# In-projection with a 512-column moving operand in the first and last token block

## The chip, the cores and the metric

The kernel runs as one program on one core of a Trainium2 chip. The metric is the device time of one execution in microseconds (us). The kernel before takes 2049.98 us, the median of three runs (2048.39 to 2051.28). One more execution was recorded by the hardware profiler, and all durations below are from that one.

## The reference

The reference is one transformer block on 2048 tokens of width 1024, with 256 context tokens. What matters here is its first part: the normed and modulated tokens are multiplied by one wide matrix `w_in`, and the product is split into eight pieces.

```python
hx = modulate(rmsnorm(x, norm1_w), sh1, sc1)
aq, ak, av, mq, mk, mv, mo, gates = jnp.split(h @ w_in, offs, -1)
mqk = jax.nn.silu(short_conv(jnp.concatenate([mq, mk], -1), conv_qk))
```

`aq`, `ak`, `av` feed a windowed attention (8 heads of 64, window 128, plus the context tokens), `mq`, `mk`, `mv`, `mo` and the gates feed a linear recurrence over chunks in both directions. Behind these come the output projection and a mixture of 16 experts of which each takes its best 256 tokens.

## The kernel before

The kernel has three stages, one behind the other: in-projection with attention (`phase_in`), recurrence with output projection (`phase_mix`), and experts (`phase_moe`). The change touches the first one alone.

**Tokens.** The tokens are worked through in four blocks of 512, and a block is two units of 256 tokens, `("x", 2b)` and `("x", 2b+1)`. The context is one more unit, worked through beside block 0. A unit's activations are held transposed (model dimension on the partitions) as two fp32r tiles of 8 x 256 columns, a rounded part `hx_hi` and the rest `hx_lo`. There are three slots for units (`self.hxs`); a unit takes the slot that came free first (`hxslot`). The units of block 0 get slots 0 and 1, those of block 1 slots 2 and 0, of block 2 slots 1 and 2, and of block 3 slots 0 and 1 again. In the kernel before each slot is a pair of tiles of its own (`hx_pair`).

**Weights.** `w_in` is loaded 128 columns at a time (L721), split by ACT into `w_hi` (L735) and by DVE into `w_lo` (L741). Each product is hi*hi, hi*lo and lo*hi, so 3 x 8 matmuls per output tile.

**Two kinds of chain.** Where the output is wanted with tokens on the partitions (`kv`, `q`, `mv`, `mo`), `tok_chain` (L758) keeps the activations stationary and moves 256 or 272 weight columns. Where it is wanted with channels on the partitions (`mk`, `mq`, which the convolution runs along the tokens), `chan_chain` (L776) keeps 128 x 128 of the weights stationary and moves the tokens of a unit, 256 columns. It does so for one unit, then for the other, into the two halves of one PSUM tile `mm` of 512 columns. So each stationary piece is loaded twice, once per unit. A block has 8 such chains for its two units (4 groups of 2), and block 0 has 4 more for the context unit. Their output goes through the convolution and a SiLU (`conv_out`).

**Order.** Nothing is left to the compiler's scheduling. All work of the stage is written as generators that ask for an engine with a cost in us (`yield "P", CH * 0.108` asks TensorE for four matmuls), and `Flow.run` plays them against one clock per engine and takes the waiting task of best priority. What comes out is a fixed sequence of instructions per engine. The engines then run their sequences strictly in that sequence and wait for each other by semaphores. The projection (`main`) has the last priority on TensorE, so that attention scores (L258, L262), transposes (L303), and values (L331, L332) are put in wherever the planner's clock says that their input is there. Planned costs of other engines are `A(n)` = 0.085 + 0.00085 n for ACT and `V(n)` = 0.07 + 0.00105 n for DVE, n being the columns.

Of the kernel before, what the change touches and what calls it, by code (L numbers as in the profile page):

```python
# [22 lines left out]
F32R = mybir.dt.float32r  # L23
# [12 lines left out]
KT = D // 128  # L36
# [320 lines left out]
class Kernel:  # L357
# [69 lines left out]
    def phase_in(self):  # L427
        nc, tc = self.nc, self.tc
        with ExitStack() as st:
            pool = lambda name, bufs, **k: st.enter_context(tc.tile_pool(name=name, bufs=bufs, **k))  # L430
            self.ps = pool("psin", 1, space=PSUM)
            self.right, self.mod, self.att = ExitStack(), ExitStack(), ExitStack()
            self.keep = self.outer.enter_context(tc.tile_pool(name="gkeep", bufs=1, side="right"))
            self.hxp = self.right.enter_context(tc.tile_pool(name="hxp", bufs=2, side="right"))
            self.hxs = [self.hx_pair(self.hxp, i) for i in range(2)]
            self.early = ExitStack()
            self.ep = self.early.enter_context(tc.tile_pool(name="early", bufs=1, side="right"))
            self.wp = pool("wring", 1)
            self.w_hi = self.wp.tile([128, 4, KT, 136], F32R, name="w_hi")
            self.w_lo = self.wp.tile([128, 4, KT, 136], F32R, name="w_lo")  # L440
            self.mp = self.mod.enter_context(tc.tile_pool(name="mod", bufs=1))
            self.pool = pool
            fl = self.fl = Flow()
            self.bufs, self.alt = BUFS, {}
            self.tok = {n: Tokens(k) for n, k in BUFS.items()}
            self.tok["hx"], self.tok["slot"] = Tokens(2), Tokens(4)
            self.hxslot = [0, 1, 2]
            self.hx = {}
            units = [("x", 0), ("x", 1), ("c", 0)] + [("x", i) for i in range(2, 8)]
            self.wm_ev = [Event() for _ in range(KT)]  # L450
            self.xn = {u: Event() for u in units}
            self.hx_ev = {u: Event() for u in units}
            self.hh_ev, self.hl_ev = ({u: [Event() for _ in range(4)] for u in units} for _ in range(2))
            self.order = {u: n for n, u in enumerate(units)}
            self.hx_freed = {u: Event() for u in units}
            self.mod_ev, self.opened, self.main_done, self.rest_ev, self.turned = (Event() for _ in range(5))
            self.att_ev, self.gt_ev = Event(), Event()
            self.reach = {(b, g): Event() for b in range(4) for g in GROUPS}
            self.w_ev = [Event() for _ in range(88)]
            self.kt_ev = [Event() for _ in range(NT)]  # L460
            self.ckt_ev = [Event() for _ in range(2)]
            self.q_ev = {(n, i): Event() for n in range(NT) for i in range(2)}
            self.unit_done = [Event() for _ in range(NT)]
            self.g_ev = Event()
            self.g_left = NT + 2
            self.q2t, self.carry = {}, {}
            fl.spawn(self.load_x(units), PRI["loadx"])
            fl.spawn(self.mod_first(), PRI["mod1"])
            for u in units:
                fl.spawn(self.make_hx(u), PRI["hx"])  # L470
            fl.spawn(self.weights(), PRI["w"])
            fl.spawn(self.main(), PRI["main"])
            self.uns = [Unit(self, n, kv) for n in range(NT) for kv in range(2)]
            fl.spawn(self.scores_flow(), PRI["sc"])
            fl.spawn(self.trans_flow(), PRI["tr"])
            fl.spawn(self.values_flow(), PRI["val"])
            fl.spawn(self.mod_rest(), PRI["modr"])
            fl.spawn(self.gates(), PRI["gates"])
            fl.run()
            self.early.close()  # L480
            self.right.close()
# [282 lines left out]
    def chan_chain(self, sl, units):  # L764
        yield self.tok["mm"]
        ps = self.buf(self.ps, "mm", [128, 512])
        for j, u in enumerate(units):
            hi, lo, _ = self.hx[u]
            i = 0
            for w, hx, evs in ((self.w_hi, hi, self.hh_ev), (self.w_hi, lo, self.hl_ev), (self.w_lo, hi, self.hh_ev)):  # L770
                for k in range(KT):
                    if k % CH == 0:
                        for ev in evs[u][k // 2:(k + CH + 1) // 2]:
                            yield ev
                        yield "P", CH * 0.108
                    self.nc.tensor.matmul(ps[:, j * 256:(j + 1) * 256], lhsT=w[:, sl, k, 0:128], rhs=hx[:, k, :],  # L776
                                          start=(i == 0), stop=(i == 23))
                    i += 1
        return ps
# [1998 lines left out]
```

## Time and profile before

| | |
|---|---|
| Median of three runs | 2049.98 us |
| Profiled execution, its own time | 2041.91 us |
| Its span, first to last instruction | 2040.1 us |
| TensorE busy | 1854.6 us (91%) |
| VectorE (DVE) busy | 1597.8 us (78%) |
| ScalarE (ACT) busy | 1281.9 us (63%) |
| GpSimd (POOL) busy | 855.1 us (42%) |
| In-projection and attention | about 44 to 910 us of the span |
| Recurrence and output projection | about 910 to 1490 us |
| Experts | about 1490 to 2040 us |

The profiled execution took 8.07 us less than the median of the runs. Busy is a sum over instructions, with overlaps counted once; matmuls are pipelined, and the end of one is modelled, so the start of one to the start of the next tells their pace better than their length. An engine's idle time costs something only where it delays the chain of work that ends last.

### The profile page before, as it was taken

The page shows a single profiled execution, that of the slowest core. Times are in us where ns is not written, and L with a number is a line of the kernel's source. Part 1 is how long each engine was busy: PE and PEld are TensorE (multiplying, and loading weights), DVE is VectorE, ACT ScalarE, POOL GpSimd, SP SyncE. Part 2 cuts the span into 40 slices and gives each one's busy share as a digit, 9 for nine tenths or more (in the row PEclk, how much of TensorE's full clock was granted, in tenths as well). Part 3 has the DMA queues.
Part 4 walks back from the last instruction along what each step waited for, and adds up shares of the span by engine and source line. Part 5 has one row for each costly group of instructions (what it writes and reads, how often), then busy time and mean ns, then how long its engine had stood idle before and what let it go on. Part 6 is the DMA issues. An engine that isn't in the chain of part 4 may idle for free.

```text
span 2040.1 us, 36979 instructions
## 1 busy us (share of the span) xinstructions
PE 1854.6 (91%) x12921; PEld 1657.3 (81%) x12921; DVE 1597.8 (78%) x3470; ACT 1281.9 (63%) x3136; POOL 855.1 (42%) x828
## 2 busy tenths in 40 slices
PE   8799999999999999987989798993499999999997
PEld 2698998899889989985777576782399999999996
DVE  3799789998998799868999777756777878787772
ACT  3567777777787777775656488864355545454542
POOL 0324324433443243225778765413244535353532
PEclk9899999999999999997999899996699999999999
DMA  8343264445432333237878677636277878878772
GB/s 281 101 146 102 71 194 119 126 139 152 114 108 79 94 83 102 77 99 226 267 254 274 237 252 242 220 132 240 74 232 216 262 222 257 238 235 253 225 230 42
DMA packets 293498, 357.81 MB, mean 175 GB/s; under 512 B 27288, under 2 KB 225592, under 8 KB 292416
## 3 DMA queue, kind: packets, MB, share of 16 engines
q1 hardware_dynamic: 283072, 320.32, 49.7%
q0 software_dynamic: 9376, 34.08, 7.2%
q8 instruction: 102, 1.67, 0.4%
q10 hardware_dynamic: 864, 1.05, 0.1%
q14 instruction: 84, 0.69, 0.1%
HBM read 270.73 MB, written 84.54 MB: 174 GB/s over the span
## 4 chain that ended last, share of the span: by engine, by line
PE 58%; DVE 21%; ACT 7%; DMA 6%; issue 5%; POOL 1%; SPq 0%; POOLq 0%; DVEq 0%; ACTq 0%
PE gu L2637 18%; PE mm L758 9%; PE yp L2689 8%; PE po L2002 5%; DVE w_lo L741 3%; DMA w_raw<-in_w_in 2%; PE t L303 2%; PE h L1910 2%; PE s L258 2%; PE o L593 1%; PE o L332 1%; PE t L2581 1%; PE o L331 1%; ACT w_hi L735 1%; PE h L1622 1%
## 5 line engine op out<-in xcount | busy, mean ns | idle before, releaser
L2486 ACT ACTIVATE ew_hi<-ew_raw 128x1024 fp32r<-128x1024 f32 x192 | 202.1, 1056 | 155.7 <-PE yp L2689 91.7
L2446 DVE TENSOR_TENSOR ew_lo<-ew_raw,ew_hi 128x1024 fp32r<-128x1024 f32 x152 | 217.5, 1440 | 33.2 <-issue 17.9
L291 POOL TENSOR_SCALAR P<-P,am 128x640 f32<-128x640 f32 (+1 forms) x128 | 112.8, 881 | 258.5 <-DVE am L289 147.7
L741 DVE TENSOR_TENSOR w_lo<-w_raw,w_hi 128x256 fp32r<-128x256 f32 (+1 forms) x352 | 156.9, 471 | 30.5 <-ACT w_hi L735 28.6
L2709 POOL DMA_INDIRECT out_x<-y,idx x32 | 57.1, 1786 | 271.0 <-DVE y L2703 183.8
L2637 PE MATMUL gu<-xg_hi,ew_hi 128*128 128x256 f32 x1024 | 148.5, 283 | 0.0
L735 ACT ACTIVATE w_hi<-w_raw 128x256 fp32r<-128x256 f32 (+1 forms) x352 | 134.9, 410 | 19.8 <-DMA w_raw<-in_w_in 19.0
L758 PE MATMUL mm<-w_hi,hx_hi 128*128 128x256 f32 (+1 forms) x944 | 142.7, 289 | 4.8 <-ACT hxr L933 2.2
L758 PE MATMUL mm<-w_lo,hx_hi 128*128 128x256 f32 (+1 forms) x944 | 141.2, 286 | 0.0
L758 PE MATMUL mm<-w_hi,hx_lo 128*128 128x256 f32 (+1 forms) x944 | 140.9, 287 | 0.0
L2637 PE MATMUL gu<-xg_hi,ew_lo 128*128 128x256 f32 x1024 | 140.8, 279 | 0.0
L2637 PE MATMUL gu<-xg_lo,ew_hi 128*128 128x256 f32 x1024 | 140.7, 279 | 0.0
L758 PEld LDWEIGHTS mm<-w_hi,hx_hi 128*128 128x128 f32 x944 | 125.0, 190 | 9.1 <-ACT hxr L933 2.6
L2637 PEld LDWEIGHTS gu<-xg_hi,ew_hi 128*128 128x128 f32 x1024 | 131.2, 189 | 0.1
L2637 PEld LDWEIGHTS gu<-xg_hi,ew_lo 128*128 128x128 f32 x1024 | 128.4, 188 | 0.0
L2637 PEld LDWEIGHTS gu<-xg_lo,ew_hi 128*128 128x128 f32 x1024 | 128.4, 188 | 0.0
L758 PEld LDWEIGHTS mm<-w_hi,hx_lo 128*128 128x128 f32 x944 | 124.0, 189 | 3.3 <-issue 2.6
L758 PEld LDWEIGHTS mm<-w_lo,hx_hi 128*128 128x128 f32 x944 | 124.3, 189 | 1.8 <-issue 0.9
L314 DVE TENSOR_TENSOR pl<-t,ph 128x512 fp32r<-128x512 f32 x156 | 105.8, 684 | 24.3 <-ACT ph L312 23.0
L282 ACT ACTIVATE P<-s,am 128x640 f32<-128x640 f32 (+1 forms) x128 | 99.8, 780 | 31.0 <-DVE am L280 25.6
L2703 DVE SCALAR_TENSOR_TENSOR y<-yp,gv,g2b 128x512 f32<-128x512 f32 x64 | 48.0, 751 | 89.8 <-PE yp L2689 89.8
L280 DVE CUSTOM_DVE_ANT_0 s<-s,mrow,nsink 128x640 f32<-128x640 f32 (+1 forms) x120 | 105.3, 878 | 12.9 <-PE s L262 6.6
(480 smaller groups left out, 5613.0 us busy)
## 6 DMA issues: line engine op xcount, KB each, us to landing
w_raw<-in_w_in SPq DMA_DIRECT2D x176, 256.0 KB
ew_raw<-in_w_gate SPq DMA_DIRECT2D x32, 1024.0 KB
ew_raw<-in_w_up SPq DMA_DIRECT2D x32, 1024.0 KB
ew_raw<-in_w_down SPq DMA_DIRECT2D x32, 1024.0 KB
xt<-in_w_mod SPq DMA_DIRECT2D x64, 256.0 KB
out_x<-xl SPq DMA_DIRECT2D x32, 512.0 KB
s_vs<-vsl SPq DMA_DIRECT2D x16, 516.0 KB
vsl<-s_vs SPq DMA_DIRECT2D x16, 516.0 KB
```

What stands on the lines that cost most here:

```text
L280: nc.vector.tensor_tensor_reduce(x, x, mask, 1.0, k.nsink[:, h:h + 1], op0=OP.add, op1=OP.min, accum_out=m[:, 0:1])
L282: nc.scalar.activation(P[:, :n], sc, AF.Exp, bias=m[:, 0:1], scale=-1.0, accum_out=m[:, 1:2])
L291: nc.gpsimd.tensor_scalar(P[:, :n], P[:, :n], m[:, 4:5], 0.0, op0=OP.mult, op1=OP.add)
L314: nc.vector.tensor_sub(lo, pt, f(hi))
L735: nc.scalar.activation(hi, raw[:, k:k + 2, :n], AF.Copy)
L741: nc.vector.tensor_sub(lo, raw[:, k:k + 2, :n], f(hi))
L758: self.nc.tensor.matmul(ps[:, :2 * n].rearrange("p (a b) -> p a b", a=2), lhsT=hx[:, k, t * 128:(t + 1) * 128], rhs=w[:, sl:sl + 2, k, :n] ...
L2002: self.nc.tensor.matmul(po, lhsT=m[:, k, :], rhs=self.wo[k0 + k][wi][:, sl], start=(j == 0), stop=(j == 11))
L2446: (self.nc.vector if eng == "D" else self.nc.gpsimd).tensor_sub(out, x, y)
L2486: nc.scalar.activation(hi[:, sl], raw[:, sl], AF.Copy)
L2637: nc.tensor.matmul(po[:, ft, :], lhsT=w[:, k, ft * 128:(ft + 1) * 128], rhs=x[:, k, :], start=(j == 0), stop=(j == 23))
L2689: nc.tensor.matmul(po[hf], lhsT=hs[i][h][:, ft, t * 128:(t + 1) * 128], rhs=wd[i][w][:, ft, hf * 512:(hf + 1) * 512], start=(j[hf] == 0), ...
```

## The change

The two slots 0 and 1 become one tile, `hx01`, indexed by slot, by part (0 is hi, 1 is lo), by k and by token; `self.hxs` holds views of it, so all writers and the other chains work as they did. `chan_chain` gets a branch for the case that its two units sit in slots 0 and 1, which is so in block 0 and block 3. There one matmul moves 512 columns, 256 from each slot, over one stationary piece: 24 matmuls of 512 columns in place of 48 of 256. The planner is asked for two such matmuls at a time at a cost of 0.46 us, where it was asked for four at 4 x 0.108 = 0.432 us, and each group waits for the activations of both units. Blocks 1 and 2 and the context unit take the old branch.

```diff
-            self.hxs = [self.hx_pair(self.hxp, i) for i in range(2)]
+            self.hx01 = self.hxp.tile([128, 2, 2, KT, 256], F32R, name="hx01", bufs=1)
+            self.hxs = [(self.hx01[:, i, 0], self.hx01[:, i, 1]) for i in range(2)]
...
         ps = self.buf(self.ps, "mm", [128, 512])
+        if [self.hx[u][2] for u in units] == [0, 1]:
+            i = 0
+            for w, j, evs in ((self.w_hi, 0, self.hh_ev), (self.w_hi, 1, self.hl_ev), (self.w_lo, 0, self.hh_ev)):
+                for k in range(KT):
+                    if k % 2 == 0:
+                        for u in units:
+                            yield evs[u][k // 2]
+                        yield "P", 0.46
+                    self.nc.tensor.matmul(ps.rearrange("p (a b) -> p a b", a=2), lhsT=w[:, sl, k, 0:128],
+                                          rhs=self.hx01[:, :, j, k, :], start=(i == 0), stop=(i == 23))
+                    i += 1
+            return ps
```

Since the costs enter the planner's clock, the sequences of all engines change from the first such chain on, to the end of the stage. The two later stages keep their sequences. Lines below the branch stand 13 lines further down in the changed kernel, those between the two edits one line further.

TensorE at the first channel chains of block 0. `hx_hi` and `hx_lo` are the parts of a unit (the number behind them is the builder's: 96 and 97 unit x0, 98 and 99 unit x1, 386 and 387 the context), `mm` the PSUM tile, `hxr` and `gate` what is transposed for keys and gates. Before:

```order
L776 MATMUL mm<-hx_hi_96,w_hi 128x256 x8
L776 MATMUL mm<-hx_lo_97,w_hi 128x256 x8
L1056 MATMUL tr<-cst,hxr_734 128x128
L1057 MATMUL tr<-cst,gate 8x128
L1058 MATMUL tr<-cst,gate 8x128
L776 MATMUL mm<-hx_hi_96,w_lo 128x256 x8
L776 MATMUL mm<-hx_hi_98,w_hi 128x256 x8
L776 MATMUL mm<-hx_lo_99,w_hi 128x256 x8
L776 MATMUL mm<-hx_hi_98,w_lo 128x256 x8
L776 MATMUL mm<-hx_hi_386,w_hi 128x256 x8
```

The same place in the changed kernel, where `hx_96` is the joint tile and 383 and 384 are the context:

```order
L776 MATMUL mm<-hx_96,w_hi 128x512 x8
L1069 MATMUL tr<-cst,hxr_731 128x128
L1070 MATMUL tr<-cst,gate 8x128
L1071 MATMUL tr<-cst,gate 8x128
L776 MATMUL mm<-hx_96,w_hi 128x512 x8
L776 MATMUL mm<-hx_96,w_lo 128x512 x8
L789 MATMUL mm<-hx_hi_383,w_hi 128x256 x8
```

Six groups of eight matmuls of 256 columns became three groups of eight of 512. The key transposes stand behind as many projected columns as before.

TensorE later in block 0, at the first scores over three key tiles (L258 with 384 columns), that is of the attention's second tile of 128 queries. Before:

```order
L758 MATMUL mm<-w_hi,hx_lo_99 128x256 x4
L996 MATMUL tr<-cst,hxr_1804 128x128 x2
L758 MATMUL mm<-w_hi,hx_lo_99 128x256 x4
L758 MATMUL mm<-w_lo,hx_hi_98 128x256 x8
L258 MATMUL s<-kt,q2t 128x384 x2
L262 MATMUL s<-ckt,q2t 128x256 x2
L758 MATMUL mm<-w_hi,hx_hi_386 128x256 x8
```

And in the changed kernel:

```order
L789 MATMUL mm<-hx_lo_384,w_hi 128x256 x4
L1009 MATMUL tr<-cst,hxr_1685 128x128 x2
L789 MATMUL mm<-hx_hi_383,w_lo 128x256 x8
L759 MATMUL mm<-w_hi,hx_96 128x256 x8
L258 MATMUL s<-kt,q2t 128x384 x2
L262 MATMUL s<-ckt,q2t 128x256 x2
L759 MATMUL mm<-w_hi,hx_96 128x256 x8
```

Before, this score stands in the `mv` chains of unit x1, and 912 projection matmuls of 256 columns stand ahead of it in the row; in the changed kernel it stands in those of unit x0, and 824 stand ahead, a matmul of 512 columns counted as two.

TensorE at the end of the stage; L1449 (L1462 in the changed kernel) is the first matmul of the next stage. Before:

```order
L303 MATMUL t<-cst,P 128x128 x4
L331 MATMUL o<-ph,vt 128x512
L332 MATMUL o<-pl,vt 128x512
L303 MATMUL t<-cst,P 128x128 x4
L758 MATMUL mm<-w_lo,hx_hi_98 128x256 x8
L331 MATMUL o<-ph,cvt 128x512
L332 MATMUL o<-pl,cvt 128x512
L331 MATMUL o<-ph,cvt 128x512
L332 MATMUL o<-pl,cvt 128x512
L1449 MATMUL t<-wr,sh_82 1x16 x8
```

In the changed kernel:

```order
L759 MATMUL mm<-w_lo,hx_96 128x256 x4
L331 MATMUL o<-ph,cvt 128x512
L332 MATMUL o<-pl,cvt 128x512
L759 MATMUL mm<-w_hi,hx_96 128x256 x16
L759 MATMUL mm<-w_lo,hx_96 128x256 x8
L759 MATMUL mm<-w_hi,hx_96 128x256 x16
L759 MATMUL mm<-w_lo,hx_96 128x256 x8
L1462 MATMUL t<-wr,sh_82 1x16 x8
```

Before, the last values of the attention end the row; in the changed kernel 48 projection matmuls (the last two `mo` chains) stand behind them.

## Rows read from the trace of the kernel before

**Rows 1.** The page's head and its summary of engines: busy time, share of the span, instructions.

```profile
span 2040.1 us, 36979 instructions
PE 1854.6 (91%) x12921; PEld 1657.3 (81%) x12921; DVE 1597.8 (78%) x3470; ACT 1281.9 (63%) x3136; POOL 855.1 (42%) x828
```

**Rows 2.** Busy time of each engine in stretches of the stage, cut by token block (95 to 310, 310 to 521, 521 to 722 and 722 to 910 us); columns as in the first line.

```profile
core 0: us, PE busy (x) PEld busy (x) DVE busy (x) ACT busy (x) POOL busy (x), PEclk, DMA share, GB/s
95.00:310.00 215.00, 206.49 (x1621) 196.08 (x1620) 182.77 (x477) 155.98 (x427) 71.72 (x114) 1.00 0.44 129
310.00:521.00 211.00, 199.98 (x1540) 186.69 (x1541) 193.44 (x504) 160.50 (x430) 80.23 (x106) 1.00 0.46 131
521.00:722.00 201.00, 193.34 (x1496) 183.30 (x1495) 171.66 (x457) 158.67 (x429) 77.72 (x105) 1.00 0.36 100
722.00:910.00 188.00, 181.05 (x1376) 168.58 (x1374) 161.94 (x451) 143.69 (x371) 60.51 (x93) 1.00 0.29 83
```

**Rows 3.** The same view for the two stretches in which the channel chains of blocks 0 and 3 run (95 to 178 and 722 to 809 us) and for the rest of these blocks.

```profile
95.00:178.00 83.00, 78.03 (x631) 73.65 (x630) 77.31 (x197) 58.56 (x161) 27.96 (x50) 1.00 0.47 136
178.00:310.00 132.00, 128.46 (x993) 122.43 (x992) 105.47 (x281) 97.42 (x268) 43.77 (x64) 1.00 0.42 124
...
722.00:809.00 87.00, 83.17 (x653) 77.41 (x651) 83.84 (x239) 67.02 (x175) 31.30 (x49) 1.00 0.36 100
809.00:910.00 101.00, 97.88 (x723) 91.17 (x723) 78.10 (x214) 76.67 (x196) 29.21 (x44) 1.00 0.23 68
```

**Rows 4.** The chain of work that ended last, its shares by line: in 95 to 178 us, in 722 to 809 us, and in 809 to 910 us.

```profile
by line: DVE w_lo L741 16.6%; issue 9.8%; DMA s_mq<-cv 8.2%; DMA xt<-in_x 5.3%; ACT w_hi L735 5.2%; DVE cv L876 4.1%; DMA w_raw<-in_w_in 3.9%; DVE cv L874 3.4%; DVE s L280 2.6%; DVE cu L549 2.4%; ACT cu L543 2.4%; ACT cu L545 2.3%; DVE cv L
...
by line: PE mm L776 13.7%; DVE w_lo L741 11.8%; issue 11.0%; DVE cv L876 4.7%; DVE s L280 4.1%; DVE pl L314 3.5%; DVE q2t L1006 3.5%; ACT w_hi L735 3.2%; DVE grow L1277 3.1%; ACT P L282 2.9%; DVE cv L874 2.7%; DVE cu L549 2.0%; DVE am L287 
...
by line: PE mm L758 34.9%; PE t L303 13.0%; PE s L258 8.5%; PE o L331 7.1%; PE o L332 6.9%; DMA s_att<-cv 5.5%; PE s L262 5.2%; DMA w_raw<-in_w_in 3.4%; issue 2.7%; ACT P L282 1.9%; ACT w_hi L735 1.4%; DVE w_lo L741 1.3%; ACT cv L347 1.2%; 
```

**Rows 5.** What TensorE waited for, all of 44 to 910 us: total, times, longest.

```profile
PE s L258 <- ACT P L282: 7.9, 14, 1.4
...
PE o L332 <- DVE pl L314: 4.3, 8, 1.0
PE tr L996 <- DVE q2t L1006: 4.2, 4, 2.5
```

**Rows 6.** All channel-chain matmuls, by part: count, ns of one (least, median, most), first and last start.

```profile
L776 PE MATMUL mm<-hx_hi,w_hi x544: 274/280/387, 95.2 to 806.6; 128*128 128x256 f32 x182
L776 PE MATMUL mm<-hx_lo,w_hi x544: 275/280/388, 96.2 to 807.5; 128*128 128x256 f32 x182
L776 PE MATMUL mm<-hx_hi,w_lo x544: 274/280/388, 98.7 to 808.7; 128*128 128x256 f32 x182
```

**Rows 7.** TensorE in order of time: start, length, instructions merged. Channel chains of 256 columns in block 0, with nothing between them.

```profile
99.73 1.11 PE L776 MATMUL mm<-hx_hi,w_hi 128*128 128x256 f32 x8
...
105.38 1.10 PE L776 MATMUL mm<-hx_hi,w_hi 128*128 128x256 f32 x8
```

**Rows 8.** The same view, matmuls of 512 columns: in this stage (attention values), in the next one (output projection), and in the experts (24 in a row, the first and the last shown).

```profile
906.70 0.39 PE L331 MATMUL o<-ph,cvt 128*128 128x512 f32 x1
906.94 0.40 PE L332 MATMUL o<-pl,cvt 128*128 128x512 f32 x1
907.17 0.39 PE L331 MATMUL o<-ph,cvt 128*128 128x512 f32 x1
907.40 0.43 PE L332 MATMUL o<-pl,cvt 128*128 128x512 f32 x1
...
945.42 1.10 PE L2002 MATMUL po<-wo_hi,mixh 128*128 128x512 f32 x4
946.36 1.09 PE L2002 MATMUL po<-wo_hi,mixl 128*128 128x512 f32 x4
...
1813.81 0.39 PE L2689 MATMUL yp<-ew_hi,h_hi 128*128 128x512 f32 x1
...
1819.02 0.39 PE L2689 MATMUL yp<-ew_lo,h_hi 128*128 128x512 f32 x1
```

**Rows 9.** The same view, token chains, whose moving operand of 256 columns is read in two pieces of 128.

```profile
785.58 1.11 PE L758 MATMUL mm<-w_hi,hx_lo 128*128 128x256 f32 x8
...
787.49 1.11 PE L758 MATMUL mm<-w_hi,hx_hi 128*128 128x256 f32 x8
```

**Rows 10.** Groups of DVE and ACT instructions over 60 to 920 us: line, engine, operation, shapes, count, busy us, mean ns of one, idle time before them.

```profile
L741 DVE TENSOR_TENSOR w_lo<-w_raw,w_hi 128x256 fp32r<-128x256 f32 x312 | 139.2, 472 | 11.8 <-ACT w_hi L735 10.0
L735 ACT ACTIVATE w_hi<-w_raw 128x256 fp32r<-128x256 f32 x312 | 118.8, 409 | 15.7 <-DMA w_raw<-in_w_in 14.9
```

**Rows 11.** The chain that ended last, at the end of the stage: start, us, what.

```profile
905.91 0.97 PE mm L758 x8
906.90 0.40 ACT moe L912
...
908.30 0.60 ACT cv L347
...
909.73 5.56 DMA s_att<-cv
```

## The prediction

> **What bounds the kernel now.** I read the page's summary first: over the whole span TensorE is the busiest engine, 1854.6 of 2040.1 us, with VectorE behind it at 1597.8 [rows 1]. An average over three stages says little about one of them, so I next cut the in-projection by token blocks [rows 2]. In all four blocks TensorE is busy 95 to 96% of the time, and the granted clock is 1.00, the 2.4 GHz level; what it is not busy is 8.5 us in block 0, 11.0 in block 1, 7.7 in block 2 and 6.95 in block 3. So over a block TensorE is the bound, and a matmul saved is worth something as long as the idle time does not grow in its place.
>
> Inside blocks 0 and 3 the picture splits [rows 3]. While the channel chains run, DVE is as full as TensorE: 77.3 against 78.0 of 83 us in block 0, and 83.8 against 83.2 of 87 us in block 3. In the rest of the blocks TensorE is busy 97% and DVE 77 to 80%. The chain of waits says the same thing [rows 4]. In the channel stretch of block 0 the channel matmuls L776 are not among its large shares at all; the weight split on DVE leads with 16.6%. In that of block 3 they have 13.7%, which is 11.9 of 87 us. In the last stretch TensorE's lines lead, L758 alone with 34.9%. So the matmuls that the change touches stand mostly beside work of DVE that ends later. Their saving shows up only by letting TensorE reach the later work, where it is the bound, sooner.
>
> **The change part by part.** *Fewer, wider matmuls.* There are 544 x 3 = 1632 channel matmuls [rows 6]. Of these 4 x 24 = 96 are the context's, and 1536 are the four blocks', 384 each. Blocks 0 and 3 have 768, which become 384 of 512 columns; 384 weight loads go with them. Columns stay the same. From start to start a 256-column matmul of these chains takes (105.38 - 99.73) / 48 = 0.1177 us [rows 7], two of them 0.2354. For 512 columns there are three rows [rows 8]: the values in this stage (907.40 - 906.70) / 3 = 0.2333 us; the output projection (946.36 - 945.42) / 4 = 0.235 us; the experts (1819.02 - 1813.81) / 23 = 0.2265 us. None of them reads its 512 columns in two pieces. The token chains read theirs in two, and take (787.49 - 785.58) / 16 = 0.1194 us [rows 9], 0.0017 more than a channel matmul. Best end: the experts' pace and no surcharge, 0.2354 - 0.2265 = 0.0089 us a pair, times 384 = 3.4 us gained. Worst end: the output projection's pace with the surcharge, 0.2367, 0.5 us lost. The values are the nearest row by their surroundings, the experts by their form (a long run, each with weights of its own), so I take the middle of those two, 0.230, with the surcharge: 0.2316, 0.0038 us a pair, 1.5 us gained.
>
> The weight loads that go are not on the path by these rows: all 512-column rows have one load each and still run near twice the pace of 256. The Trainium skill says more than one thing of this ("TensorE: Matmul & The Clock Gate", section "Back-to-back issue gap"): an isolated gap of N/2.4 + 2.5 ns, by which a pair would gain 2.5 ns and the change 1.0 us, and a sustained 131 ns per matmul of 512 columns in a stream of load and matmul pairs. The trace contradicts the second: none of the 512-column paces above is under 226 ns. The first agrees with it in size only: 256 columns take 117.7 ns here, where it gives 109.
>
> *The joint tile.* It takes the room of the four tiles, and its writers write the same slices. Waits that would tie slot 0's writers to slot 1's readers cost nothing in blocks 0 and 3, where both slots are filled before the chains start; block 1 and 2 fill one of them while the other is read. I take nothing for it, as every write into a slot stands in the sequence behind the chains that planned to free it; were this wrong it would add to TensorE's waits of [rows 5], and belongs to the slower rival's price.
>
> *Waiting for both units.* A group now needs hi or lo of both. The `kv` and `q` chains of both units stand ahead of the first channel chain, so both have been read in full by then: nothing.
>
> *Another sequence.* This is the larger term, and its sign is open. A channel chain was planned at 48 x 0.108 = 5.18 us and ran 48 x 0.1177 = 5.65; it is now planned at 24 x 0.23 = 5.52 and would run 24 x 0.2316 = 5.56. The planner thus sees TensorE later than it did by 0.34 us a chain, 5.4 us over 16 chains, and puts attention work in ahead of more projection. The score shown in the change stands behind 824 projection matmuls, not 912, and at the stage's end 48 stand behind the last values, where none stood. Does that cost idle time? The four blocks are four sequences of much the same work, and their idle times [rows 2] have a mean of 8.5 and a standard deviation of 1.8 us. If all four are drawn anew the sum moves by 3.6 us (1.8 times the root of 4). I take zero, with that spread. No DMA is added or dropped, and on SP's queue the weight loads (w_raw) keep their places among the other transfers but for a few, so nothing is taken for them; they end 3.9% of the chain in block 0's stretch [rows 4].
>
> *The stage's end.* Before, the end runs from the last token chain (905.91 + 0.97) over the sigmoid and the values' store to 909.73, and the store takes 5.56 us more, after which loads of the next stage are free to go [rows 11]. Now `mo` chains end the row. Their sigmoid starts on ACT right behind the chain, as in those rows, and their store some 3 us behind it, as the values' store does there. The values' store then lies some 48 x 0.1194 = 5.7 us ahead of the end and no longer ends it: between 0 and 2 us gained, taken as nothing since a store ends the stage either way.
>
> Sum: -1.5 us. The profiled execution's own 2041.91 would be 2040.4. It stood 8.07 us under the median of the runs, so the sum is carried to the median as a difference: 2049.98 - 1.5 = 2048.5 us.
>
> **The rivals.** *Slower: attention comes too early for DVE.* The planner's DVE is too fast: a weight split is planned at 0.07 + 256 x 0.00105 = 0.34 us and takes 0.472, on ACT 0.30 and 0.409 [rows 10]. Before, TensorE's plan for these chains was too fast as well, by 9%, and this hid the error. Now it is nearly right, and attention pieces stand up to 88 matmuls earlier, 88 x 0.1177 = 10.4 us, while DVE has 83 - 77.3 = 5.7 us to spare in block 0. In block 3, with the 48 matmuls of the end as the measure, 5.7 us against 3.2 to spare. What DVE can't take, 4.7 + 2.5 = 7.2 us, becomes waits of TensorE at L258, L332 and L996, the places where it waits for ACT and DVE now [rows 5], with the projection queued behind them. Then 7.2 - 1.5 = +5.7 us: 2055.7. It decides from 5.6 us more waits on, where 1.5 us are paid back and 4.1 remain. Against it: longest waits there are 1.0 to 2.5 us now, and projection pieces stand between.
>
> *Faster: the sequence fits better.* Since TensorE's plan now holds in these stretches, ACT and DVE meet it where they expect it. If blocks 0 and 3 lost half of their 8.5 + 6.95 us of idle time, that is 7.7 us, and 1.5 with it: 2040.8. For it speaks the chain in block 0's stretch, where TensorE is not what ends last, so earlier attention can start DVE's work earlier. Against it speaks that DVE has little to spare there.
>
> *The weight load sets the pace.* If a matmul cost by its load and not by its columns, one of 512 would take the 0.1177 us of one of 256 [rows 7], and 384 x 0.1177 = 45 us would go: 2005. All rows of 512 columns speak against it [rows 8]. The Trainium skill's 131 ns (the section named above) would be nearly this, some 40 us; the trace does not bear it out.
>
> **How the numbers follow.** 0.2% of this kernel is 4.1 us; less cannot be told from no change. The neutral case (forecast) has 0.44, slower 0.28, faster 0.27, the load 0.01. The neutral case is -1.5 with a spread of 3.6: 24% of it is faster by over 4.1, 6% slower, 70% within. Faster: 0.44 x 0.24 + 0.27 x 0.9 + 0.01 = 0.36. Slower: 0.44 x 0.06 + 0.28 x 0.85 = 0.27. The remaining 0.37 is within. The forecast's own range is 2044 to 2053, with 1.3 spreads on each side. The range for 8 in 10 reaches to both rivals, 2040.8 and 2055.7, and past them by what the pair's bounds add (1.9 us below, 2.0 above): 2039 to 2058.
>
> **What would show it.** Right: 384 matmuls of 512 columns in the channel chains with starts 0.226 to 0.237 us apart, 768 fewer instructions on TensorE and its loads, the stage's last values some 6 us ahead of its last projection, and the stage's last matmul (907.40 us before [rows 8]) within 5 us of where it stood. The slower rival shows as TensorE idle time of over 13 us in block 0 with DVE as releaser; the faster one as idle time under 5. The forecast is wrong if the pace of 512 columns lies outside those bounds, or if the time changes in the two later stages, whose sequences are the same.

## The result and the profile after

The changed kernel is slower. Its median is 2065.37 us in five runs (2063.2 to 2072.64), beside 2049.98 us in five runs of the kernel before (2045.0 to 2052.54): a ratio of 1.0089 [1.007, 1.0109], or 15.4 us between the medians. The time lies above the range predicted. The profiled execution took 2063.79 us of its own.

First the head of the page and its summary of engines, to be read against [rows 1]:

```profile
span 2062.0 us, 36216 instructions
PE 1869.4 (91%) x12537; PEld 1645.6 (80%) x12537; DVE 1602.5 (78%) x3470; ACT 1285.4 (62%) x3136; POOL 857.3 (42%) x828
```

The edit did what it says: TensorE issues 384 matmuls fewer (12537 for 12921), and 384 weight loads fewer. Yet it is busy longer, and the share of the span is the same 91%. This average can't say where the time went, so the next view is busy time by token block, cut where the first channel chain of each block starts and, at the end, where the last projection ends.

```profile
core 0: us, PE busy (x) PEld busy (x) DVE busy (x) ACT busy (x) POOL busy (x), PEclk, DMA share, GB/s
97.10:316.60 219.50, 207.78 (x1415) 184.97 (x1413) 180.15 (x470) 156.07 (x422) 73.68 (x112) 0.99 0.43 125
316.60:530.50 213.90, 200.35 (x1548) 187.85 (x1547) 195.69 (x497) 160.57 (x428) 78.13 (x105) 1.00 0.47 133
530.50:736.00 205.50, 196.47 (x1498) 184.02 (x1498) 175.44 (x471) 162.33 (x435) 79.07 (x107) 1.00 0.34 96
736.00:925.50 189.50, 182.02 (x1187) 157.03 (x1185) 162.53 (x445) 141.73 (x365) 58.39 (x90) 1.00 0.26 75
```

Cut in the same way, the blocks before took 214.7, 211.1, 201.3 and 184.7 us (95.2 to 907.0; the cuts of [rows 2] are rounded), 811.8 in all. Now it is 828.4. Every block is longer, by 4.8, 2.8, 4.2 and 4.8 us, blocks 1 and 2 too, whose matmuls the edit leaves alone. TensorE's idle time is 11.7, 13.6, 9.0 and 7.5 us, 41.8 in all; before, by these cuts, it was 8.5, 11.0, 7.7 and 4.8, or 32.0. So 9.8 of the 16.6 us show as idle time, and 6.8 within the busy time, where short stalls between pipelined matmuls can hide.

The stretches with the channel chains (97 to 190 and 736 to 829 us) and the rest of those blocks answer to [rows 3]:

```profile
97.00:190.00 93.00, 85.16 (x474) 69.03 (x473) 85.49 (x217) 65.94 (x177) 34.86 (x56) 0.98 0.48 137
190.00:316.00 126.00, 122.12 (x941) 115.89 (x940) 94.16 (x254) 89.85 (x245) 38.30 (x56) 1.00 0.40 117
...
736.00:829.00 93.00, 87.19 (x490) 69.42 (x489) 89.50 (x257) 71.31 (x186) 33.32 (x53) 1.00 0.32 89
829.00:926.00 97.00, 94.96 (x699) 87.61 (x697) 73.03 (x189) 70.75 (x181) 25.56 (x39) 1.00 0.20 61
```

The channel stretches grew from 83 and 87 us to 93 each, and the rest shrank from 132 and 101 to 126 and 97. In block 0's channel stretch DVE does 85.5 us of work where it did 77.3, and in the rest of the block 94.2 where it did 105.5: work was drawn into the stretch in which DVE was as full as TensorE already. The chain that ended last there, and in block 3's, answers to [rows 4]:

```profile
by line: DVE w_lo L742 12.9%; DMA w_raw<-in_w_in 8.2%; issue 7.9%; DVE s L280 4.0%; DMA xt<-in_x 3.8%; DVE q2t L1019 3.7%; DVE cv L889 3.5%; PE mm L776 3.4%; DVE cv L887 3.3%; DMA xt<-in_w_mod 3.2%; POOL ropeu L972 3.0%; DVE cv L885 3.0%; D
...
by line: issue 15.7%; DVE w_lo L742 13.7%; DVE s L280 6.2%; DVE cv L889 5.4%; DVE q2t L1019 5.1%; DMA w_raw<-in_w_in 4.4%; DMA s_mq<-cv 3.5%; DVE grow L1290 3.3%; DVE pl L314 3.1%; DVE cv L885 2.8%; ACT P L282 2.7%; PE mm L776 2.5%; DVE cv 
```

The share of the channel matmuls (now L776 for the wide ones) fell from 13.7% to 2.5% in block 3. "Issue" (11.0 to 15.7%) and DVE's lines fill the place. Of the latter, the weight split's share rose in block 3 and fell in block 0, and the attention's scores (DVE s L280) rose from 2.6% to 4.0% and from 4.1% to 6.2%. What TensorE waited for, from 44 to 926 us, answers to [rows 5]:

```profile
PE s L258 <- ACT P L282: 14.6, 23, 1.7
PE o L332 <- DVE pl L314: 7.8, 10, 2.0
...
PE tr L1009 <- DVE q2t L1019: 2.3, 4, 1.3
```

The first two waits grew from 7.9 to 14.6 and from 4.3 to 7.8 us. Both are waits of attention matmuls for the attention's own softmax (`P` is its exponentials, `pl` the lower half of its split). Of the 10.2 us by which they grew, 8.1 fall in blocks 1 and 2, where they are 16.2 us together and were 8.1.

The wide matmuls themselves, in order of time, to be read against [rows 7, 8]:

```profile
177.98 3.91 PE L776 MATMUL mm<-hx,w_hi 128*128 128x512 f32 x16
181.73 0.63 PE L776 MATMUL mm<-hx,w_lo 128*128 128x512 f32 x2
```

From start to start that is (181.73 - 177.98) / 16 = 0.234 us, where two of 256 columns took 0.2354. The end of the stage, by the chain that ended last, answers to [rows 11]:

```profile
919.91 5.73 PE mm L759 x48
925.66 0.39 ACT moe L925
...
927.97 5.03 DMA s_mo<-moe
...
933.58 6.13 DMA xl<-in_w_out
```

And the first output projection of the next stage, before and after; it closes the first stage and what follows on it directly, and is the measure used below. Before:

```profile
939.25 2.08 PE L2002 MATMUL po<-wo_hi,mixh 128*128 128x512 f32 x4 [4.23 <-ACT mixh L1594]
```

After:

```profile
957.02 2.08 PE L2015 MATMUL po<-wo_hi,mixh 128*128 128x512 f32 x4 [3.68 <-ACT mixh L1607]
```

It starts 17.8 us later: the first channel chain 1.9 us later (97.1 for 95.2 us), and from there to the first output projection it is 859.9 us in place of 844.0. From the first output projection to the end of the span it is 1100.8 us before and 1105.0 after; that part has the same sequence in all kernels here, and took 1099.7 to 1110.7 us in their profiles. So the loss lies in the first stage, and a few us of any single profile's span are not the change's: the two profiled executions are 21.9 us apart, the medians 15.4.

### The profile page after: what moved, and what is told of

Same layout as the page of the kernel before. It is cut to its first block, busy times and chain, and to the rows that moved or that the text cites. A ratio compares the mean times of both kernels' runs of the same rounds, so it can differ in the third digit from the quotient of the medians.

```text
span 2062.0 us, 36216 instructions
## 1 busy us (share of the span) xinstructions
PE 1869.4 (91%) x12537; PEld 1645.6 (80%) x12537; DVE 1602.5 (78%) x3470; ACT 1285.4 (62%) x3136; POOL 857.3 (42%) x828
## 4 chain that ended last, share of the span: by engine, by line
PE 56%; DVE 22%; ACT 8%; issue 6%; DMA 6%; POOL 1%; SPq 0%; POOLq 0%; DVEq 0%; ACTq 0%
PE gu L2650 17%; PE mm L759 9%; PE yp L2702 8%; PE po L2015 5%; DVE w_lo L742 3%; DMA w_raw<-in_w_in 2%; PE t L303 2%; PE h L1923 1%; PE o L594 1%; PE s L258 1%; PE t L2594 1%; PE o L332 1%; PE o L331 1%; DVE s L280 1%; PE h L1635 1%
## 5 line engine op out<-in xcount | busy, mean ns | idle before, releaser
L2459 DVE TENSOR_TENSOR ew_lo<-ew_raw,ew_hi 128x1024 fp32r<-128x1024 f32 x152 | 217.4, 1440 | 33.2 <-issue 17.9
L759 PE MATMUL mm<-w_hi,hx 128*128 128x256 f32 (+1 forms) x1344 | 190.9, 288 | 3.0 <-ACT hxr L946 1.9
L742 DVE TENSOR_TENSOR w_lo<-w_raw,w_hi 128x256 fp32r<-128x256 f32 (+1 forms) x352 | 167.3, 498 | 30.1 <-ACT w_hi L736 28.9
L759 PEld LDWEIGHTS mm<-w_hi,hx 128*128 128x128 f32 x1344 | 173.0, 190 | 6.9 <-ACT hxr L946 2.4
L312 ACT ACTIVATE ph<-t 128x512 fp32r<-128x512 f32 x156 | 92.0, 594 | 39.0 <-PE t L303 36.6
L280 DVE CUSTOM_DVE_ANT_0 s<-s,mrow,nsink 128x640 f32<-128x640 f32 (+1 forms) x120 | 105.2, 877 | 12.3 <-PE s L262 8.5
L2459 POOL TENSOR_TENSOR ew_lo<-ew_raw,ew_hi 128x1024 fp32r<-128x1024 f32 x40 | 98.9, 2478 | 31.5 <-ACT ew_hi L2499 31.2
L2618 ACT ACTIVATE xv<-t,sh,sc 128x256 f32<-128x256 f32 x128 | 67.9, 562 | 62.6 <-PE t L2594 62.6
L759 PE MATMUL mm<-w_lo,hx 128*128 128x256 f32 (+1 forms) x672 | 100.4, 287 | 0.0
```

Source lines behind the costliest of these rows:

```text
L280: nc.vector.tensor_tensor_reduce(x, x, mask, 1.0, k.nsink[:, h:h + 1], op0=OP.add, op1=OP.min, accum_out=m[:, 0:1])
L742: nc.vector.tensor_sub(lo, raw[:, k:k + 2, :n], f(hi))
L759: self.nc.tensor.matmul(ps[:, :2 * n].rearrange("p (a b) -> p a b", a=2), lhsT=hx[:, k, t * 128:(t + 1) * 128], rhs=w[:, sl:sl + 2, k, :n] ...
L2459: (self.nc.vector if eng == "D" else self.nc.gpsimd).tensor_sub(out, x, y)
```

## The experiments

Three theories stood against each other at first: the new sequence costs the time (S), the wide matmul itself does (W), or the joint tile ties the two slots together by waits (J). The first three runs part them.

**The joint tile alone.** The branch is taken out, so all engines have the sequences of before.

```diff
-        if [self.hx[u][2] for u in units] == [0, 1]:
...
-            return ps
```

> The joint tile hx01 alone; the channel chains stay as before (256 columns, one unit after the other), and every engine has the sequence of the kernel before. If the new sequence is what costs (theory S), or the wide matmul itself (theory W): no change, within 0.2% of 2050 us. If waits between the two slots of the joint tile cost (theory J): most of the 15 to 22 us, so 2060 us or more, with TensorE or DVE waits at the writers of hx01 (L667, L671, L674).

Measured: 2051.95 us beside 2046.42, ratio 1.0018 [1.0005, 1.003]. First output projection at 940.2 us. At most a small part of the loss, so J falls.

**Wide matmuls at the old planned cost.** TensorE keeps the wide matmuls; the other engines have the sequences of before.

```diff
-                        yield "P", 0.46
+                        yield "P", CH * 0.108
```

> Joint tile and matmuls of 512 columns, but the planner is asked for 0.432 us per group, as it was for four matmuls of 256; all other engines have the sequence of the kernel before, and TensorE the same but for the wider matmuls. Theory S: no loss, and the gain of the matmuls alone, 384 x 0.002 to 0.004 = 1 to 1.5 us, so 2046 to 2051 us. Theory W: 2060 us or more. Theory J: 2060 us or more.

**Narrow matmuls at the new planned cost.** In place of the branch's own loop, four matmuls of 256 columns, unit after unit, planned at 0.46; the sequences are those of the changed kernel.

```diff
+            for s, u in enumerate(units):
...
+                        if k % CH == 0:
...
+                            yield "P", 0.46
+                        self.nc.tensor.matmul(ps[:, s * 256:(s + 1) * 256], lhsT=w[:, sl, k, 0:128], rhs=hx[:, k, :],
+                                              start=(i == 0), stop=(i == 23))
```

> Joint tile and the old matmuls of 256 columns, unit after unit, but the planner is asked for 0.46 us per group of four; all engines have the sequence of the changed kernel, TensorE but for the narrower matmuls. Theory S: as slow as the changed kernel, 2063 to 2069 us. Theory W: as the kernel before, 2048 to 2052 us. Theory J: 2060 us or more, as in the first of these three.

Measured: wide at the old cost 2049.32 us beside 2046.42, ratio 1.0017 [1.0001, 1.0033]; narrow at the new cost 2062.92, ratio 1.0089 [1.0069, 1.011], the changed kernel's own ratio without one wide matmul. The same two kernels by block, blocks 0 to 2 of the first and blocks 0 and 2 of the second. Wide, old cost:

```profile
96.80:314.50 217.70, 207.36 (x1426) 186.98 (x1424) 181.62 (x474) 155.35 (x425) 73.91 (x113) 0.99 0.43 126
314.50:525.50 211.00, 200.11 (x1542) 186.71 (x1541) 193.81 (x505) 159.84 (x430) 81.51 (x106) 1.00 0.45 131
525.50:725.60 200.10, 193.65 (x1498) 183.50 (x1497) 170.90 (x457) 158.83 (x429) 77.77 (x105) 1.00 0.35 101
```

Narrow, new cost:

```profile
99.60:319.40 219.80, 207.39 (x1607) 195.47 (x1605) 180.33 (x470) 155.93 (x422) 74.78 (x112) 0.99 0.43 125
...
532.60:736.50 203.90, 196.19 (x1498) 184.00 (x1498) 175.06 (x471) 162.45 (x435) 78.48 (x107) 1.00 0.34 97
```

Block 2 is 200.1 us with the old sequence and 203.9 with the new, as it was 201.3 and 205.5; the form of the matmul doesn't matter. Block 0 parts them less, 217.7 against 219.8, and the four blocks together take 812.6 and 825.2. The first output projection starts at 942.2 and at 957.9 us. S stands, W falls: the wide matmuls at the old cost and the changed kernel differ by the number 0.46 in the planner's cost alone.

**Which part of the sequence?** Now the question was why. S1: the planner's DVE is too fast, so attention is put in before DVE can serve it. S2: any new sequence is a draw, good or bad by chance. S3: GpSimd's tensor operations collide with DVE's weight splits (last section). Four other costs were planned for a pair of wide matmuls, all else as in the changed kernel.

```diff
-                        yield "P", 0.46
+                        yield "P", 0.40
```

and 0.444, 0.48 and 0.50 in the same place.

> The changed kernel, with 0.40 us in place of 0.46 as the planned cost of a group of two wide matmuls. Attention scores then stand on the mean 19 projection matmuls later in TensorE's row than before, not 17 earlier. Theory S1 (attention too early for DVE costs, so the loss grows with the planned cost): no loss, 2040 to 2050 us. Theory S2 (each sequence is a new draw, no trend with the planned cost): anything from 2045 to 2070 us. Theory S3 (the loss is DVE time that weight splits spend against GpSimd): the time follows the weight splits' total on DVE, 166 us in the fast sequence and 175 in the slow one.

> The changed kernel with a planned cost of 0.444 us. The sequence follows the changed kernel in block 0 and the kernel before nearly in block 3. S1: between the two, 2052 to 2062 us. S2: anything from 2045 to 2070 us. S3: by the weight splits' total on DVE, 166 us for 2047, 175 us for 2063.

> The changed kernel with a planned cost of 0.48 us. In blocks 1 and 2 the scores stand where they stood before; in blocks 0 and 3 they stand earlier, by up to 80 and 32 projection matmuls. S1: as slow as the changed kernel or slower, 2063 us or more, the loss in blocks 0 and 3 alone. S2: anything from 2045 to 2070 us. S3: by the weight splits' total on DVE.

> The changed kernel with a planned cost of 0.50 us; scores stand on the mean 20 projection matmuls earlier, in block 0 up to 100. S1: slower than the changed kernel, 2066 us or more. S2: anything from 2045 to 2070 us. S3: by the weight splits' total on DVE.

| planned cost of a pair | ratio | first output projection, us |
|---|---|---|
| 0.40 | 0.9997 [0.9981, 1.0014] | 941.8 |
| 0.432 (the run above) | 1.0017 [1.0001, 1.0033] | 942.2 |
| 0.444 | 1.0095 [1.0074, 1.0116] | 958.5 |
| 0.46 (the change) | 1.0089 [1.007, 1.0109] | 957.0 |
| 0.48 | 1.0109 [1.0092, 1.0126] | 956.4 |
| 0.50 | 1.0116 [1.0099, 1.0133] | 964.0 |

This is a step between 0.432 and 0.444, with two like values below it and four above. A draw for each sequence would rarely fall so; S2 is unlikely. S1 missed too: it expected the loss to grow with the cost, 2052 to 2062 us at 0.444, where the median is 2066.7. The step's sharpness is not explained by any run. At 0.48 the blocks read:

```profile
96.50:323.00 226.50, 209.09 (x1422) 186.13 (x1421) 180.57 (x473) 155.90 (x424) 75.96 (x114) 0.99 0.41 122
323.00:533.60 210.60, 201.73 (x1546) 187.66 (x1545) 195.61 (x505) 160.20 (x431) 86.20 (x106) 1.00 0.44 131
533.60:733.60 200.00, 193.28 (x1499) 183.50 (x1498) 171.31 (x458) 158.42 (x429) 77.45 (x105) 1.00 0.36 101
733.60:922.90 189.30, 181.59 (x1180) 156.59 (x1180) 161.81 (x446) 142.36 (x367) 57.80 (x91) 1.00 0.27 76
```

Here blocks 1 and 2 are as before, and the loss is in blocks 0 and 3, where the edited chains are: 11.8 and 4.6 us. This execution was the fastest of four (2060.1 us beside a median of 2069.1), so where the others lost 9 us more is not seen. DVE's weight splits, 352 in all, are busy 157.6 us here and 157.9 at 0.50, against 156.9 before and 167.3 in the changed kernel. The loss comes without the longer splits, so S3 falls as its cause.

**A truer plan for DVE.** If S1 holds, planning the weight split at what it takes [rows 10] must take the loss away while the cost 0.46 stays. First both engines of the split, in the changed kernel and in the one before:

```diff
-            yield A(2 * n)
+            yield "A", 0.41
...
-                yield V(2 * n)
+                yield "D", 0.47
```

> The changed kernel with the planned cost 0.46 us kept, but with the weight split planned at what the trace shows: 0.47 us on DVE instead of 0.34 and 0.41 on ACT instead of 0.30. Scores then stand on the mean 41 projection matmuls later than before, values 70 later. S1 (attention put in earlier than DVE can feed it, because DVE is planned too fast): most of the loss goes, 2045 to 2054 us. S2 (a new draw): anything from 2045 to 2070 us.

> The kernel before (no wide matmuls, planned cost 0.432) with the weight split planned at 0.47 us on DVE and 0.41 on ACT. The control for the run with both: scores 55, values 73 matmuls later. S1: no loss, 2042 to 2050 us. S2: anything from 2045 to 2070 us.

Measured: the changed kernel with it 2038.86 us, ratio 0.9962 [0.9946, 0.9978], faster than both, and faster than S1 expected; the kernel before with it 2044.34 beside 2046.32, ratio 0.9987 [0.9967, 1.0008], no change that can be told. The 15 us and more are gone. In the profiled execution of the faster kernel the first channel chain starts at 92.2 us and the first output projection at 933.5, 841.3 us later (859.9 in the changed kernel, 844.0 before); of the 5.8 us by which it leads the kernel before there, 3.0 are its earlier start.

**One block's chains at 0.46, the other's at 0.432.**

```diff
-                        yield "P", 0.46
+                        yield "P", 0.46 if units[0] == ("x", 0) else CH * 0.108
```

and the reverse.

> The changed kernel with the planned cost of 0.46 us in block 0 alone; in block 3 it is 0.432, so that block 3's attention ends where it did before. S1: the loss of block 0 and its neighbours stays, that of block 3 (5 us) goes: 2056 to 2062 us. S2: anything from 2045 to 2070 us.

> The changed kernel with the planned cost of 0.46 us in block 3 alone; blocks 0 to 2 have the sequence of the kernel before. S1: the loss of block 3 alone or less, as only some values there stand earlier (up to 140 matmuls): 2048 to 2055 us. S2: anything from 2045 to 2070 us, with all of the difference behind 722 us.

Measured: block 0 alone at 0.46 gives 1.0065 [1.0044, 1.0085], block 3 alone 1.0045 [1.0025, 1.0065]. Together that is 1.011, near the whole 1.0089, so each brings part. With block 0's choice the first output projection is at 954.8 us, with block 3's alone at 944.2, though the latter profiled execution was the fastest of ten (2046.2 us beside a median of 2055.2). Block 0's choice also moves what follows. Blocks 0 to 2 with it:

```profile
96.60:317.50 220.90, 208.05 (x1415) 185.03 (x1413) 180.32 (x470) 155.74 (x421) 72.27 (x112) 0.99 0.42 125
317.50:530.50 213.00, 201.78 (x1548) 189.29 (x1547) 195.43 (x497) 160.57 (x428) 78.20 (x105) 0.99 0.46 134
530.50:735.80 205.30, 196.35 (x1498) 184.02 (x1498) 175.23 (x471) 162.47 (x435) 78.94 (x107) 1.00 0.34 97
```

Against the wide matmuls at the old cost (217.7, 211.0 and 200.1 us, above), from which it differs up to there by block 0's cost alone, that is 3.2 us more in block 0 and 7.2 more in blocks 1 and 2.

**Which engine's plan, and which matmul?** The faster version with narrow matmuls; then DVE's true cost alone; then ACT's alone.

```diff
-                yield V(2 * n)
+                yield "D", 0.47
```

> The sequence of the run with the truer weight split (planned 0.47 us on DVE, 0.41 on ACT, 0.46 for a group of the channel chains), but with channel matmuls of 256 columns, unit after unit. If the wide matmul is worth nothing beyond 384 x 0.002 to 0.004 us: within 4 us of that run, 2037 to 2043 us. If the wide matmul brought the gain: 2044 us or more.

> The changed kernel with the weight split planned truly on DVE alone (0.47 us); ACT's is left at 0.30. Scores stand on the mean 47 projection matmuls later than before, but the first of block 0 up to 112 earlier. If DVE's plan is the cause: most of the loss goes, 2040 to 2052 us, and what is left lies in block 0. If ACT's: 2060 us or more.

> The changed kernel with the weight split planned truly on ACT alone (0.41 us); DVE's is left at 0.34. Scores stand on the mean 18 projection matmuls later than before, but in blocks 0 and 3 some stand 40 to 120 earlier, values up to 300. If DVE's plan is the cause: the loss of blocks 0 and 3 stays, 2056 us or more. If ACT's: 2040 to 2052 us.

Measured: narrow 2039.31 us, ratio 0.9959 [0.9941, 0.9978], the same as wide: the wide matmul is worth nothing that can be told in the good sequence either. DVE alone 2056.31, ratio 1.0042 [1.0025, 1.006], where S1 expected less than the kernel before: a miss. ACT alone 1.0064 [1.0047, 1.0081]. The miss is in a place that the theory hadn't looked at. With DVE's plan alone the first channel chain starts at 115.0 us, not 97.1, and the stretch ahead of it and the blocks read:

```profile
44.00:115.00 71.00, 50.29 (x297) 42.72 (x297) 42.91 (x137) 31.99 (x102) 14.25 (x22) 0.72 0.27 80
115.00:326.50 211.50, 202.55 (x1402) 183.53 (x1402) 173.86 (x447) 151.33 (x407) 68.23 (x108) 1.00 0.44 128
...
736.70:911.50 174.80, 171.79 (x1133) 150.32 (x1132) 151.67 (x423) 133.76 (x348) 58.56 (x86) 1.00 0.28 78
```

In that first stretch TensorE waits for DVE at the transposes of the first units, one of them for 3.51 us, and its granted clock is 0.72 on average (0.86 in the changed kernel from 44 to 97.1 us):

```profile
78.76 1.09 PE L690 MATMUL tr<-cst,xt 128*128 128x128 f32 x4 [3.51 <-DVE gatet L1091]
```

The four blocks take 796.5 us together up to the last projection (115.0 to 911.5), but here attention work stands behind it, the last value at 927.96. So the fair measure is up to the first output projection:

```profile
953.10 2.08 PE L2015 MATMUL po<-wo_hi,mixh 128*128 128x512 f32 x4 [3.67 <-ACT mixh L1607]
```

From the first channel chain that is 838.1 us, 5.9 fewer than before and 21.8 fewer than in the changed kernel, but the chain starts 17.9 us later than there. So S1's gain was there, and a worse order in the start-up ate most of it. That is a claim which a run can test: keep the old plan for the weights of the start, and the true one behind it. `s` counts the 128-column pieces of the weights, 22 to a block.

```diff
-                yield V(2 * n)
+                yield V(2 * n) if s < 6 else ("D", 0.47)
```

and the same with `s < 12`.

> The changed kernel with the weight split planned at 0.47 us on DVE from the seventh column group of w_in on (0.34 before it); ACT's is left at 0.30. Scores stand on the mean 67 projection matmuls later than in the kernel before. If DVE's too fast plan is the cause of the loss: the first channel chain starts at 95 to 98 us, the four blocks take 796 to 806 us against 811 in the kernel before, so 2032 to 2043 us. If it is not: 2055 us or more.

> The same from the thirteenth column group on; in block 0 the scores stand up to 32 matmuls earlier than in the kernel before, behind it as in the run with DVE planned truly throughout. If DVE's plan is the cause: blocks 1 to 3 as in that run (212, 198 and 175 us), block 0 between 215 and 220 us, so 2036 to 2047 us. If it is not: 2055 us or more.

Measured: 2040.55 us beside 2049.61 for 6, ratio 0.9964 [0.9945, 0.9982], and 2043.72 for 12, ratio 0.9968 [0.9951, 0.9986]. Both are faster than the kernel before, with nothing but DVE's planned cost altered in the changed kernel. The blocks for 6:

```profile
98.50:311.10 212.60, 204.21 (x1410) 183.73 (x1409) 176.29 (x459) 154.43 (x418) 71.73 (x110) 1.00 0.43 126
311.10:511.30 200.20, 193.82 (x1510) 183.64 (x1508) 183.89 (x496) 156.28 (x426) 81.57 (x109) 0.99 0.44 130
511.30:722.60 211.30, 203.33 (x1538) 189.22 (x1538) 184.96 (x487) 164.22 (x438) 77.30 (x106) 1.00 0.36 106
722.60:898.20 175.60, 172.23 (x1147) 153.31 (x1146) 155.08 (x427) 136.43 (x356) 54.44 (x86) 1.00 0.29 83
```

They start at nearly the same time as in the changed kernel and take 799.7 us in place of 828.4 up to the last projection; here too values stand behind it, up to 909 us. TensorE's idle time is 28.7 us with them (26.1 without), in place of 41.8. To the first output projection at 933.67 it is 835.2 us in place of 859.9. The two waits that had grown are back, from 44 to 898 us at 8.3 us in 12 waits and 3.4 in 8 (up to 910 us the second is 4.2 in 12).

```profile
PE s L258 <- ACT P L282: 8.3, 12, 1.9
...
PE o L332 <- DVE pl L314: 3.4, 8, 0.6
```

## Why the prediction was wrong

**What bounds the kernel: right.** The channel stretches are DVE's as much as TensorE's, and TensorE's saving did not shorten them: with the attention work that moved in they grew by 10 and 6 us.

**Fewer, wider matmuls: right in kind, a third of its size.** The pace is 0.234 us where 0.2316 was taken, within its bounds 0.2265 to 0.2367; a pair gains 0.0014 us, 0.5 us over 384 in place of 1.5. The times can't tell 0.5 us from 1.5, but wide against narrow makes no difference in either sequence (1.0017 and 1.0018; 0.9962 and 0.9959). The sustained 131 ns that the Trainium skill gives for 512 columns ("TensorE: Matmul & The Clock Gate", section "Back-to-back issue gap") is not reached by this form either; its isolated gap of 216 ns is the nearer one to 234.

**The joint tile and the wait for both units: nearly right.** Nothing was taken, and the runs allow 0.05 to 0.3% for the tile; the wide branch in the old sequence adds nothing to that.

**Another sequence: wrong, and this step made nearly the whole miss.** It was taken as zero with a spread of 3.6 us, from the scatter of idle time over the four blocks before [rows 2]. It measured +16.6 us over the blocks. A spread of 3.6 is small even for a draw: the sum before is one draw too, so the difference of two has 1.8 times the root of 8, or 5.1, and 16.6 is over three of these. The fault is in the reasoning: four blocks planned with one set of costs show how idle time scatters under that set. Another set can shift them to the same side, as it did all four in the changed kernel, and such a shift is no draw around zero.

**The slower rival had the mechanism, and less than half of its size.** It named the cause, a planner's DVE that is too fast for attention placed earlier once TensorE's plan is nearly true; the runs with DVE's true cost bear that out. It priced 7.2 us from DVE's spare time in the channel stretches of blocks 0 and 3 alone [rows 3]. In the changed kernel blocks 1 and 2 lost 7.0 us more, and the rival had no term for them. They inherit it from block 0: with block 0's chains alone at 0.46 they are nearly as long as in the changed kernel (213.0 and 205.3 us for 213.9 and 205.5). That is not so at every cost, as at 0.48 they lost nothing in the profiled execution. Its visible sign, over 13 us of idle time in block 0, did not come in the changed kernel: 11.7 (at 0.48 it is 17.4), and the largest releaser by name was ACT's `P` with 3.3 us, which has DVE's score step (L280) ahead of it on the chain. A mark set on one block and one releaser was too narrow. What moves is not attention's mean place alone either: with ACT's true cost alone the scores stand 18 matmuls later than before on average, and the time is 0.64% longer.

**The faster rival came true only with a truer DVE.** It expected 2040.8 us because TensorE's plan now holds. With DVE's plan true as well, and the start-up not made worse by it, the kernel runs 2038.9 to 2043.7, whether its matmuls are wide or narrow; with DVE's plan true throughout and ACT's left it runs 2056.3. That is the rival's idea in another kernel than the one it was priced for.

**The stage's end: right.** Values end 5.7 us ahead of the last projection (919.91 + 5.73 in the chain above), and the store of `mo` ends the stage. From the end of the stage's last matmul to the first output projection it is 31.4 us after (925.64 to 957.02) and 31.4 before (907.83, the last value's 907.40 + 0.43 of [rows 8], to 939.25).

**The signs.** The pace, the 768 instructions fewer on TensorE and its loads, and the values ahead of the last projection came as said. The stage's last matmul did not stay within 5 us: it ends 17.8 us later (925.64 for 907.83). What was to count against the forecast, another pace or other times in the later stages, did not come; the length of the blocks, where the miss lies, was not on that list.

**What stays open.** Why the step between 0.432 and 0.444 is so sharp; the 0.17% of the first two experiments, whose lower bounds lie near zero; how the loss falls on each block, which rests on one profiled execution for each kernel; and which waits carry it. The runs show that the planned costs make the loss and take it away. That it runs through the two attention waits is not shown for every cost: at 0.48, with a loss as large, they are 10.1 and 5.7 us, where the changed kernel has 14.6 and 7.8.

## What to carry to other kernels

Where a planner's costs set the order, a changed cost is a change of its own: run the edit with the old cost, and the new cost with the old code, before the edit is judged. A cost that becomes truer for one engine can make things worse as long as another engine's is still wrong, so correct those of the engines that share a bound together, and look at the start-up as well as at the steady blocks. Idle time that scatters under one plan said nothing here on how far another plan would shift it.

## What was not expected of the hardware

**A DVE weight split beside GpSimd.** The median split takes 0.42 us in both kernels. These two of the changed kernel take far longer, and GpSimd works on tensors at the same time. DVE in order of time, and GpSimd in the same stretch:

```profile
182.59 0.96 DVE L742 TENSOR_TENSOR w_lo<-w_raw,w_hi 128x256 fp32r<-128x256 f32 x1
...
183.76 1.50 DVE L742 TENSOR_TENSOR w_lo<-w_raw,w_hi 128x256 fp32r<-128x256 f32 x1
...
182.09 1.17 POOL L974 TENSOR_TENSOR hxr<-hxr,ropew 128x256 f32<-128x256 f32 x1
183.69 1.28 POOL L896 TENSOR_TENSOR cv<-cv,cu 128x512 f32<-128x512 f32 x1 [0.43 <-ACT cu L552]
```

Each of these splits starts while a GpSimd operation runs and ends 0.3 us behind its end (183.55 behind 183.26, 185.26 behind 184.97). The Trainium skill has this as a lock on a port that both engines share, for a DVE operation with two inputs in SBUF against a GpSimd operation that reads SBUF, where the later one waits ("SBUF — State Buffer", section "SBUF: two separate sides"); the order of the ends here agrees with it. Over the stage the splits' mean rose from 472 to 501 ns, but at 0.48 and 0.50 the kernel is as slow without that.

**A short wait and TensorE's clock.** In 160 to 164 us of the changed kernel the granted clock is 0.70 on average, a mixture of the two levels of 1.2 and 2.4 GHz, behind a wait of 2.14 us for GpSimd; two matmuls of 512 columns then start 0.43 us apart (163.58 to 164.01), where they otherwise do 0.234 apart. That is about 0.2 us lost on each such matmul in these few us, on top of the wait.

```profile
160.00:164.00 4.00, 3.32 (x16) 3.04 (x17) 3.97 (x10) 2.66 (x7) 2.10 (x3) 0.70 0.81 254
```

```profile
160.68 0.77 PE L303 MATMUL t<-cst,P 128*128 128x128 f32 x5 [2.14 <-POOL P L291]
...
163.58 0.63 PE L331 MATMUL o<-ph,vt 128*128 128x512 f32 x1
164.01 0.63 PE L332 MATMUL o<-pl,vt 128*128 128x512 f32 x1
```
